# Keys and values of the memory tokens moved from the first attention's filler to the head of a two-block kernel

## The chip, the cores and the metric

The kernel runs on one core of one Trainium2 chip. The metric is the device time of one execution in microseconds (us); of several runs the median counts.

## What is computed

Two transformer blocks follow each other on 512 tokens of width 1024, in float32. The first block has a sliding-window attention with sinks (8 heads), a sparse attention with compressed keys (8 heads), gates, and a convolved feed-forward part. The second block attends to its own tokens in two ways and to 256 memory tokens in a third. Only that third branch touches the memory input, and its keys and values depend on nothing else in the kernel:

```
def mem_branch(mq, mem, mem_norm_g, w_mem_kv, qn_g, kn_g):
    kv = rms_norm(mem, mem_norm_g) @ w_mem_kv
    k = rms_norm(kv[..., :MEM_W].reshape(b, m, MEM_HEADS, MEM_D), kn_g)
    v = kv[..., MEM_W:].reshape(b, m, MEM_HEADS, MEM_D)
```

So the memory keys and values can be made at any time before the second block needs them; the kernel stores them to DRAM and reads them back late. The first block starts with `h = rmsnorm(x, norm_mix)` and products of `h` with parts of one wide weight `w_in`.

## The kernel before

Each float32 product is made as three products of rounded halves. `split` (L97 to L108) and `wsplit` (L125 to L131) round a tile to a high part H on ACT and put the rest L on DVE; `mm3` (L191 to L198) issues H·H, L·H and H·L on TensorE (PE). A weight is loaded by the queue of SP into a tile `raw` (two buffers), and split into `wH` and `wL` (three buffers each) in pieces of 128x1024. A `raw` buffer is free again when the last of its pieces is split.

`block1` (L391) begins with the norm of x: four loads of 512 KB, one square on ACT for each (L411), a short inverse root on DVE (`rsqrt`, L267 to L274), scaling (L414 to L418), 32 transposes on PE (L422), and eight splits into `hH` and `hL` (L107, L108). The transposes use the PSUM tags T, S and O, with two buffers each. Then come three products in a row: the window keys (`dense` at L498), the window queries (L504, four output tiles of 24 matmuls) and the values (`values`, L437). Ahead of the values `mem_load` (L1170) loads the memory (1 MB), takes its norm and transposes it through the tag T alone, 16 transposes and eight splits of 256 columns.

Then `pipeline` (L161) runs the eight window heads. A step of it weaves the scores and the softmax of head i (`swa_a`, L532) with the transposes and the value product of head i-1 (`swa_b`, L571), and with `RS` steps of a filler, `fill1` (L624). A filler step is mostly one `mm3`. The filler begins with `mem_kv` (L1190): 96 matmuls of 256 columns (keys, then values), the norm of the keys, 16 transposes and nine stores. After it come the products of `w_in` for the sparse attention, each with its evacuation, and the two compressions (`compress`, L653).

In the program, a priority scheduler sets each engine's order at build time; every engine then works through its own fixed list and waits on semaphores. The order of the text sets the priorities.

Of the kernel before, what the change touches and what calls it, by code (L numbers as in the profile page):

```python
# [10 lines left out]
F32 = mybir.dt.float32  # L11
# [9 lines left out]
D = 1024  # L21
# [11 lines left out]
POOLL = 14  # L33
RS = 9
RN = 5
# [43 lines left out]
class Build:  # L79
# [76 lines left out]
    @staticmethod  # L156
    def drain(g):
        for _ in g:
            pass

    def pipeline(self, units, filler, rate, extra=(), pool=0):  # L161
# [229 lines left out]
    def block1(self):  # L391
        nc, a, tc, ctx = self.nc, self.a, self.tc, self.ctx
        W = self.rows(a["w_in"][0])
        K8 = [(0, 8)]
# [4 lines left out]
        HH = [hH[:, k] for k in range(8)]  # L399
        HL = [hL[:, k] for k in range(8)]  # L400
        x = a["x"][0].rearrange("(b p) c -> p b c", p=128)
        with tc.tile_pool(name="xp", bufs=1, side="right", reuse_waits="tile") as xp:
            xt = xp.tile([128, 4, D], F32, name="xt")
            ss = xp.tile([128, 4], F32, name="ss")
            junk = xp.tile([128, D], F32, name="junk")
            for b in range(4):
                nc.sync.dma_start(xt[:, b], x[:, b])
            self.constants(xp)
            for i in range(2):
                for b in (2 * i, 2 * i + 1):  # L410
# [61 lines left out]
        def qevac(store):  # L472
# [8 lines left out]
            return f  # L481


        swa = ExitStack()
# [16 lines left out]
        self.leng = nc.vector  # L501
        self.bias_vectors()
        QA = []
        self.dense(W, K8, 0, 512, HH, HL, qevac(QA))  # L504
        mems = ExitStack()
        mem_pool = mems.enter_context(tc.tile_pool(name="mem", bufs=1, side="right", reuse_waits="tile"))
        self.mem_load(mem_pool)
        values()
# [115 lines left out]
        def fill1():  # L624
            yield from self.mem_kv(mem_pool)
            mems.close()
            open_nsa()
# [541 lines left out]

    def mem_load(self, p):  # L1170
        nc, a = self.nc, self.a
        self.sp = p
        mt = p.tile([128, 2, D], F32, tag="mt", name="mt", bufs=1)
        ss = p.tile([128, 2], F32, name="mss")
        self.mH = p.tile([128, 8, 256], F32R, name="memH")
        self.mL = p.tile([128, 8, 256], F32R, name="memL")
        nc.sync.dma_start(mt, a["mem_2"][0].rearrange("(b p) c -> p b c", p=128))
        for b in range(2):
# [678 lines left out]
```

## Time and profile before

| what | value |
|---|---|
| median of 3 runs | 1106.35 us (1102.1 to 1108.65) |
| the profiled execution's own time | 1101.55 us |
| its span in the trace | 1099.8 us |
| PE busy | 1041.1 us (95%), 5425 matmuls |
| DVE busy | 759.9 us (69%) |
| ACT busy | 579.4 us (53%) |
| POOL busy | 269.2 us (24%) |
| DMA traffic | 110.66 MB, mean 101 GB/s |

PE is the engine with the least idle time, but its matmuls are pipelined: a busy time of 394 ns belongs to a matmul that makes room for the next one after some 230 ns. So the distance from one start to the next is read from the timeline, and small gaps do not show as idle time. The profiled execution is faster than the median of the runs by 4.8 us.

### The profile page before, as it was taken

What the parts mean: (1) busy time and instruction counts of PE and PEld (TensorE: products, weight loads), DVE (VectorE), ACT (ScalarE), POOL (GpSimd) and SP (SyncE); (2) the same over time, 40 slices, a digit from 0 to 9 for tenths busy, and PEclk for the clock granted to TensorE, in tenths of its full rate; (3) what the DMA queues carried; (4) which work ended last, traced back from release to release, by engine and by line L of the source; (5) the groups of instructions that cost most, each with busy time, mean ns of one, the idle gap of its engine ahead of it and who ended that gap; (6) DMA issues with size and microseconds to landing.
All of it is one profiled execution on the core that took longest, in us unless ns stands there. A gap on an engine that the chain in (4) does not pass through costs nothing.

```text
span 1099.8 us, 15091 instructions
## 1 busy us (share of the span) xinstructions
PE 1041.1 (95%) x5425; PEld 872.3 (79%) x5425; DVE 759.9 (69%) x1561; ACT 579.4 (53%) x1098; POOL 269.2 (24%) x382
## 2 busy tenths in 40 slices
PE   5999999999999999999999999999999968999798
PEld 4797777878878878888888888888889957776698
DVE  6669884587872655777753477774454898989983
ACT  6557664577772444444432344445537536876540
POOL 4323134232220064000000200001420459332400
PEclk9999999999999999999999999999999989999899
DMA  6845345222114262232222423122324322264212
GB/s 184 275 114 169 101 96 144 44 49 44 49 43 115 77 183 87 77 115 80 89 80 79 153 77 114 59 83 94 110 80 130 97 58 58 62 197 144 71 64 78
DMA packets 105514, 110.66 MB, mean 101 GB/s; under 512 B 5508, under 2 KB 96362, under 8 KB 105440
## 3 DMA queue, kind: packets, MB, share of 16 engines
q1 hardware_dynamic: 101440, 99.07, 31.0%
q0 software_dynamic: 4000, 10.64, 3.2%
q8 instruction: 43, 0.70, 0.3%
q14 instruction: 31, 0.25, 0.1%
HBM read 100.75 MB, written 11.03 MB: 102 GB/s over the span
## 4 chain that ended last, share of the span: by engine, by line
PE 72%; DVE 16%; DMA 5%; ACT 4%; issue 3%; SPq 0%; POOL 0%; ACTq 0%; DVEq 0%; POOLq 0%
PE ps_mm L193 19%; PE ps_mm L197 19%; PE ps_mm L198 19%; DMA raw<-in_w_in 4%; PE ps_S L1247 3%; PE ps_T L383 3%; DVE wL L130 2%; PE ps_O L1278 1%; DVE PTL L102 1%; PE ps_O L1276 1%; DVE e L372 1%; ACT e L374 1%; DVE rt L1101 1%; ACT wH L129 1%; DVE e L1300 1%
## 5 line engine op out<-in xcount | busy, mean ns | idle before, releaser
L129 ACT ACTIVATE wH<-raw 128x1024 fp32r<-128x1024 f32 (+5 forms) x178 | 169.5, 954 | 255.8 <-PE ps_mm L197 207.0
L130 DVE TENSOR_TENSOR wL<-raw,wH 128x1024 fp32r<-128x1024 f32 (+5 forms) x150 | 166.6, 1112 | 112.1 <-ACT wH L129 111.7
L198 PE MATMUL ps_mm<-nH,wL 128*128 128x512 f32 x440 | 173.5, 394 | 5.0 <-POOL wL L130 5.0
L193 PE MATMUL ps_mm<-nH,wH 128*128 128x512 f32 x440 | 173.7, 395 | 0.0
L197 PE MATMUL ps_mm<-nL,wH 128*128 128x512 f32 x440 | 173.4, 394 | 0.0
L374 ACT ACTIVATE e<-e,mn 128x256 f32<-128x256 f32 (+5 forms) x160 | 86.4, 541 | 33.1 <-DVE mn L372 32.0
L198 PEld LDWEIGHTS ps_mm<-nH,wL 128*128 128x128 f32 x440 | 83.3, 189 | 21.9 <-POOL wL L130 5.4
L197 PEld LDWEIGHTS ps_mm<-nL,wH 128*128 128x128 f32 x440 | 83.4, 190 | 16.4
L193 PEld LDWEIGHTS ps_mm<-nH,wH 128*128 128x128 f32 x440 | 83.5, 190 | 16.2
L193 PE MATMUL ps_mm<-hH,wH 128*128 128x512 f32 x232 | 94.2, 406 | 0.5 <-DVE qy L480 0.5
L198 PE MATMUL ps_mm<-hH,wL 128*128 128x512 f32 x232 | 92.2, 398 | 0.0
L197 PE MATMUL ps_mm<-hL,wH 128*128 128x512 f32 x232 | 91.8, 395 | 0.0
L383 PE MATMUL ps_T<-ident,e 128*128 128x128 f32 x368 | 64.9, 283 | 15.4 <-DVE PTL L102 8.6
L130 POOL TENSOR_TENSOR wL<-raw,wH 128x1024 fp32r<-128x1024 f32 (+1 forms) x28 | 60.7, 2167 | 76.1 <-ACT wH L129 64.4
L101 ACT ACTIVATE PTH<-ps_T 128x512 fp32r<-128x512 f32 (+1 forms) x108 | 55.6, 529 | 31.7 <-PE ps_T L383 31.0
L383 PEld LDWEIGHTS ps_T<-ident,e 128*128 128x128 f32 x368 | 45.7, 143 | 32.9 <-DVE PTL L102 9.6
L102 DVE TENSOR_TENSOR PTL<-ps_T,PTH 128x512 fp32r<-128x512 f32 (+1 forms) x108 | 63.8, 606 | 11.3 <-ACT PTH L101 10.7
L193 PE MATMUL ps_mm<-aH,wH 128*128 128x512 f32 x176 | 69.5, 395 | 0.0
L198 PE MATMUL ps_mm<-aH,wL 128*128 128x512 f32 x176 | 69.5, 395 | 0.0
L197 PE MATMUL ps_mm<-aL,wH 128*128 128x512 f32 x176 | 69.5, 395 | 0.0
L965 POOL MEMSET cv<- 128x2 f32 x44 | 4.3, 100 | 237.0 <-DVE cc L969 230.4
L966 DVE TENSOR_TENSOR cv<-ps_mm,rB 128x512 f32<-128x512 f32 x44 | 30.3, 688 | 32.5 <-PE ps_mm L198 31.3
(547 smaller groups left out, 2544.3 us busy)
## 6 DMA issues: line engine op xcount, KB each, us to landing
raw<-in_w_ffn_in SPq DMA_DIRECT2D x20, 1024.0 KB, 5.2
raw<-in_w_in SPq DMA_DIRECT2D x16, 1024.0 KB, 7.1
raw<-in_w_in SPq DMA_DIRECT2D x16, 512.0 KB, 4.1
raw<-in_w_ffn_out SPq DMA_DIRECT2D x8, 768.0 KB, 4.6
raw<-in_w_ffn_out SPq DMA_DIRECT2D x8, 640.0 KB, 4.0
xt<-in_x SPq DMA_DIRECT2D x8, 512.0 KB, 4.9
raw<-in_w_out SPq DMA_DIRECT2D x4, 1024.0 KB, 5.3
raw<-in_w_out SPq DMA_DIRECT2D x8, 512.0 KB, 3.5
```

The source lines that it names most:

```text
L101: nc.scalar.activation(H, src, AF.Copy)
L102: nc.vector.tensor_sub(L, src, f32(H))
L129: self.nc.scalar.activation(H, raw, AF.Copy)
L130: self.leng.tensor_sub(L, raw, f32(H))
L193: ins = mm(ps, wH, xH, start=first, stop=False)
L197: mm(ps, wH, xL, start=False, stop=False)
L198: mm(ps, wL, xH, start=False, stop=last)
L372: nc.vector.tensor_tensor_reduce(e, ps, bias, op0=ALU.add, op1=ALU.min, scale=1.0, scalar=3e38, accum_out=mn)
L374: nc.scalar.activation(e, e, AF.Exp, scale=-1.0, bias=mn, accum_out=sm)
L383: nc.tensor.transpose(ps[:, 128 * i:128 * i + 128], blk, self.ident)
L966: nc.vector.tensor_tensor(v[:, 2:], ps, rB, op=ALU.mult)
L1247: nc.tensor.matmul(ps[:, :n], q[:, 128 * b:128 * b + 128], k[:, :n], start=i == 0, stop=i == len(prods) - 1)
```

## The change

The memory's load is issued ahead of the loads of x (`mem_fetch`). Its norm and the first 16 steps of `mem_kv`, which are all 96 of its matmuls, are written ahead of the norm of x. The rest of `mem_kv` (the norm of the keys, the transposes, the stores) is stepped beside the product for the window queries (`beside_`), which now comes ahead of the window keys. `fill1` starts with the products of `w_in`, and the filler's rate `RS` goes from 9 to 7 steps for each head. The pool of the memory tiles is closed before the window attention's pool opens.

```diff
-RS = 9
+RS = 7
...
+    def beside_(self, g, other):
+
+        for _ in g:
+            next(other, None)
+        self.drain(other)
...
+        mems = ExitStack()
+        mem_pool = mems.enter_context(tc.tile_pool(name="mem", bufs=1, side="right", reuse_waits="tile"))
         with tc.tile_pool(name="xp", bufs=1, side="right", reuse_waits="tile") as xp:
...
+            mt = self.mem_fetch(mem_pool)
             for b in range(4):
                 nc.sync.dma_start(xt[:, b], x[:, b])
             self.constants(xp)
+            self.mem_load(mem_pool, mt)
+            mkv = self.mem_kv(mem_pool)
+            for _ in range(16):
+                next(mkv)
...
+        self.bias_vectors()
+        QA = []
+        self.beside_(self.dense_steps(W, K8, 0, 512, HH, HL, qevac(QA)), mkv)
+        mems.close()
...
         self.leng = nc.vector
-        self.bias_vectors()
-        QA = []
-        self.dense(W, K8, 0, 512, HH, HL, qevac(QA))
-        mems = ExitStack()
-        mem_pool = mems.enter_context(tc.tile_pool(name="mem", bufs=1, side="right", reuse_waits="tile"))
-        self.mem_load(mem_pool)
         values()
...
         def fill1():
-            yield from self.mem_kv(mem_pool)
-            mems.close()
             open_nsa()
...
+    def mem_fetch(self, p):
+        mt = p.tile([128, 2, D], F32, tag="mt", name="mt", bufs=1)
+        self.nc.sync.dma_start(mt, self.a["mem_2"][0].rearrange("(b p) c -> p b c", p=128))
+        return mt
```

What this does to the order of the instructions is shown at three places.

PE, head of the program. Before, the last transposes of x (`xt`) run straight into the first products of the window keys (`hH` and `wH`):

```order
L422 MATMUL ps_T_157<-ident_84,xt_77 128x128 x4
L422 MATMUL ps_S_164<-ident_84,xt_77 128x128 x3
L422 MATMUL ps_O_171<-ident_84,xt_77 128x128 x3
L422 MATMUL ps_T_178<-ident_84,xt_77 128x128 x4
L422 MATMUL ps_S_185<-ident_84,xt_77 128x128 x4
L193 MATMUL ps_mm_220<-hH_72,wH_223 128x512
```

Now the transposes of the memory (`mt`) come first, and its products start between them:

```order
L1200 MATMUL ps_T_139<-ident_89,mt_83 128x128 x2
L435 MATMUL ps_S_343<-ident_89,xt_80 128x128
L435 MATMUL ps_O_350<-ident_89,xt_80 128x128
L435 MATMUL ps_S_364<-ident_89,xt_80 128x128
L435 MATMUL ps_O_371<-ident_89,xt_80 128x128
L1200 MATMUL ps_T_144<-ident_89,mt_83 128x128 x2
L1200 MATMUL ps_T_149<-ident_89,mt_83 128x128 x2
L199 MATMUL ps_mm_174<-wH_177,memH_104 128x256
L203 MATMUL ps_mm_174<-wL_178,memH_104 128x256
```

Four transposes of x stand there; the other 28 stand behind the 96th product of the memory.

ACT, the same part of the program. Before, the splits of x (`hH`) follow the scaling of x with one weight split between:

```order
L414 ACTIVATE xt_77<-xt_77,ss_78 128x1024
L415 ACTIVATE xt_77<-xt_77,ss_78 128x1024
L326 ACTIVATE vec_norm_mix_92<-ps_T_95 128x16
L129 ACTIVATE wH_223<-raw_221 128x1024
L107 ACTIVATE hH_72<-ps_T_136,vec_norm_mix_92 128x512
```

Now they stand behind the evacuation of the memory's values, `mkv` from `ps_mm_235`, the second and last PSUM tile of the memory's products:

```order
L1076 ACTIVATE hsq_452<-mkv_167 128x256
L129 ACTIVATE wH_527<-raw_437 128x1024
L101 ACTIVATE mkv_167<-ps_mm_235 128x4x64
L129 ACTIVATE wH_572<-raw_570 128x1024
L101 ACTIVATE mkv_167<-ps_mm_235 128x4x64
L107 ACTIVATE hH_72<-ps_T_336,vec_norm_mix_97 128x512
```

PE, first window heads. Before, the scores (L549, L550) stand between products of the memory:

```order
L198 MATMUL ps_mm_671<-wH_674,memL_437 128x256
L549 MATMUL ps_S_712<-kaH0_207,qy_326 128x258
L550 MATMUL ps_S_712<-kaL0_209,qy_326 128x258
L193 MATMUL ps_mm_671<-wH_674,memH_436 128x256
L197 MATMUL ps_mm_671<-wL_675,memH_436 128x256
```

Now the products of `h` with `w_in` stand there, with 512 columns:

```order
L561 MATMUL ps_S_908<-kaH0_655,qy_546 128x130
L562 MATMUL ps_S_908<-kaL0_657,qy_546 128x130
L561 MATMUL ps_S_916<-kaH0_655,qy_546 128x258
L562 MATMUL ps_S_916<-kaL0_657,qy_546 128x258
L199 MATMUL ps_mm_892<-hH_72,wH_895 128x512
L203 MATMUL ps_mm_892<-hL_73,wH_895 128x512
L204 MATMUL ps_mm_892<-hH_72,wL_896 128x512
```

From the second compression's last product on (L719 in the kernel before), the order on PE is the same in both programs.

## Rows read from the trace of the kernel before

**Rows 1.** Timeline of the first 20 us (start us, us, instruction [idle before]).

```profile
5.84 1.06 ACT L411 ACTIVATE junk<-xt 128x1024 f32<-128x1024 f32 x1 [0.25 <-DMA xt<-in_x]
9.62 1.06 ACT L411 ACTIVATE junk<-xt 128x1024 f32<-128x1024 f32 x1 [1.34 <-DMA xt<-in_x]
...
11.87 0.48 PE L422 MATMUL ps_T<-ident,xt 128*128 128x128 f32 x1 [3.99 <-ACT xt L414]
12.13 0.42 PE L422 MATMUL ps_S<-ident,xt 128*128 128x128 f32 x1
...
18.33 0.66 PE L422 MATMUL ps_S<-ident,xt 128*128 128x128 f32 x4
18.74 0.48 PE L193 MATMUL ps_mm<-hH,wH 128*128 128x512 f32 x1
```

**Rows 2.** A stretch of 1 us (busy us of PE, PEld, DVE, ACT, POOL; granted clock, DMA share, GB/s).

```profile
9.00:10.00 1.00, 0.00 (x0) 0.00 (x0) 0.33 (x2) 0.38 (x1) 0.78 (x5) 1.00 1.14 345
```

**Rows 3.** Instructions by tile: `mt`, then `memH` (ns min/median/max, first and last start us).

```profile
L1187 PE MATMUL ps_T<-ident,mt x16: 270/273/329, 48.7 to 55.8; 128*128 128x128 f32 x16
L1179 ACT ACTIVATE memH<-mt x2: 1063/1064/1065, 37.4 to 38.6; 128x1024 fp32r<-128x1024 f32 x2
L1183 DVE TENSOR_SCALAR mt<-mt,mss x2: 748/751/754, 44.6 to 45.3; 128x1024 f32<-128x1024 f32 x2
...
L193 PE MATMUL ps_mm<-wH,memH x32: 274/282/365, 69.8 to 84.6; 128*128 128x256 f32 x32
L107 ACT ACTIVATE memH<-ps_T,vec_norm_mix x8: 457/470/476, 50.2 to 56.3; 128x256 fp32r<-128x256 f32 x8
L108 DVE SCALAR_TENSOR_TENSOR memL<-ps_T,vec_norm_mix,memH x8: 475/482/486, 51.5 to 57.4; 128x256 fp32r<-128x256 f32 x8
```

**Rows 4.** Instructions by tile: `raw`, 0 to 50 us (columns as above).

```profile
L129 ACT ACTIVATE wH<-raw x8: 873/1054/1079, 13.0 to 48.8; 128x1024 fp32r<-128x1024 f32 x5, 128x816 fp32r<-128x816 f32 x3
L130 DVE TENSOR_TENSOR wL<-raw,wH x7: 1002/1219/1227, 24.0 to 49.7; 128x1024 fp32r<-128x1024 f32 x4, 128x816 fp32r<-128x816 f32 x3
```

**Rows 5.** Timeline of PE: first window scores, products of the memory.

```profile
69.24 0.33 PE L549 MATMUL ps_S<-kaH,qy 128*128 128x130 f32 x1
...
70.21 0.29 PE L193 MATMUL ps_mm<-wH,memH 128*128 128x256 f32 x1
70.33 0.28 PE L197 MATMUL ps_mm<-wL,memH 128*128 128x256 f32 x1
```

**Rows 6.** Timeline of PE: end of the part in which the orders differ.

```profile
172.28 0.39 PE L198 MATMUL ps_mm<-hH,wL 128*128 128x512 f32 x1
174.53 1.14 PE L719 MATMUL ps_T<-w2v,hv 128*128 128x64 f32 x8 [1.86 <-POOL hv L712]
175.48 0.48 PE L193 MATMUL ps_mm<-hH,wH 128*128 128x512 f32 x1
```

**Rows 7.** Stretches of the window heads (columns as in rows 2).

```profile
69.20:85.35 16.15, 15.68 (x130) 15.24 (x129) 13.45 (x48) 10.98 (x30) 3.00 (x7) 1.00 0.52 139
122.00:135.00 13.00, 11.04 (x55) 9.17 (x54) 8.67 (x22) 8.27 (x18) 1.04 (x2) 0.87 0.47 140
148.00:160.00 12.00, 10.03 (x57) 7.91 (x56) 8.75 (x19) 8.42 (x17) 1.66 (x1) 1.00 0.31 97
sum 106.30, PE 96.56 PEld 79.97 DVE 88.99 ACT 71.87 POOL 27.20; mean PE 10.73 PEld 8.89 DVE 9.89 ACT 7.99 POOL 3.02
```

**Rows 8.** Chain of waits, longest pieces of 69 to 176 us (start us, us, what).

```profile
119.22 7.98 DMA raw<-in_w_in
141.62 8.14 DMA raw<-in_w_in
160.96 9.73 DMA raw<-in_w_in
```

**Rows 9.** Timeline of PE, then a stretch, after the first of these loads.

```profile
129.25 0.52 PE L584 MATMUL ps_O<-PTH,V 128*128 128x256 f32 x1 [1.96 <-ACT PTH L101]
...
131.00:132.00 1.00, 1.00 (x5) 0.81 (x4) 0.40 (x3) 0.00 (x1) 0.00 (x0) 0.50 0.00 0
```

More of the change, by code (lines that the diff above doesn't have):

```diff
@@ L1167, in rope_sines, with mem_load @@
             self.tabs[n] = (cc, sn)
-    def mem_load(self, p):
-        nc, a = self.nc, self.a
+    def mem_fetch(self, p):
+        mt = p.tile([128, 2, D], F32, tag="mt", name="mt", bufs=1)
+        self.nc.sync.dma_start(mt, self.a["mem_2"][0].rearrange("(b p) c -> p b c", p=128))
+        return mt
+    def mem_load(self, p, mt):
+        nc = self.nc
         self.sp = p
-        mt = p.tile([128, 2, D], F32, tag="mt", name="mt", bufs=1)
         ss = p.tile([128, 2], F32, name="mss")
@@ L1176, in mem_load @@
         self.mL = p.tile([128, 8, 256], F32R, name="memL")
-        nc.sync.dma_start(mt, a["mem_2"][0].rearrange("(b p) c -> p b c", p=128))
         for b in range(2):
```

## The prediction

> **What bounds the kernel now.** Read the stretches first: in the window heads PE is busy 96.56 of 106.3 us, DVE 88.99 [rows 7]. From 69.24 us, the first score, to 175.48 us, where the orders of the two programs meet again [rows 5, 6], PE has the least slack, but it waits. The chain of waits names what for: three loads of weights of 7.98, 8.14 and 9.73 us [rows 8]. Each can be issued only when a `raw` buffer has been split on DVE; its own split then stands on ACT ahead of the softmax of a head, and PE waits behind that. The first such wait is 1.96 us long [rows 9]. Then read the timeline of the head: PE has nothing to do until 11.87 us, transposes x, and starts its unbroken stream of products at 18.74 us [rows 1].
>
> All the instructions of before are still there, and from L719 on PE's order is the same. So the change is worth what it does to the time at which PE reaches L719's successor, at 175.48 us before: the head, and the window stage.
>
> **The head.** Memory and x are both wanted from the queue at once. The memory's 1 MB is as much as two blocks of x, so it lands when the second block does now, near 5.8 us [rows 1]. The squares of memory and x follow on ACT in turn: six of 1.06 us, each with a read of some 0.2 us behind it, in the order memory, x, memory, x, x, x. The second one of the memory ends near 9.5 us, the last of x near 13.1 us (the waits for x's blocks fall inside). DVE's inverse root is thirteen small operations in a row, with seven of x's between: about 3.5 us, to 13 us. Two scalings of 0.75 us [rows 3] end at 14.4 us.
>
> Now the memory's transposes. They use only tag T, two buffers, so they go in four rounds of two; a round is a pair of transposes, two ACT splits of 0.47 us and two DVE splits of 0.48 us [rows 3], and the next round waits for DVE. Between rounds stand x's inverse roots and scalings, and weight splits of 1.05 us (ACT) and 1.22 us (DVE) [rows 4]. With these in their order the rounds end on DVE near 16.8, 18.9, 21.7 and 23.8 us. The first weight split is done on ACT at 18.7 us and on DVE at 20.8 us, so products begin, but run on only from 21.8 us. The weights themselves are there: memory, x and both weight chunks are 5.25 MB; at the 0.345 MB per us of [rows 2] after the first 2.6 us that is 17.8 us, and the second chunk is first used at 20 us.
>
> From 21.8 us the 96 products take 0.12 us each [rows 5], 11.5 us, to 33.4 us. I add 1.7 us for the clock: PE idles for more than 2 us between the rounds, and after an idle of 1.96 us the kernel before ran at a granted clock of 0.50, the 1.2 GHz level [rows 9]. The mean of 0.87 over 13 us [rows 7] makes that 13 x 0.13 / 0.5 = 3.4 us at half speed, a loss of 1.7 us. The start of the trace reads otherwise: a transpose at 12.13 us takes 0.42 us, the last ones before 18.74 us take 0.27 us and start 0.13 us apart, (0.66 - 0.27) / 3 [rows 1]. PE had done nothing but transposes in between, so I read there a rise out of the slow level, though the granted column says 1.00 throughout.
>
> The Trainium skill, "TensorE: Matmul & The Clock Gate", in Part 4 on the transpose, says that the full clock does not engage for transposes; by it the first products are slow after any number of transposes, and the 1.7 us stand. By the trace's start, a dense row of transposes would have saved them, and the sum would be 1.7 us lower. The measurement goes against the rule there; I keep the 1.7 us for the gaps alone.
>
> So the products end at 35.1 us. ACT then has two evacuations of the memory's values (0.39 us each, an estimate from the 0.47 us of [rows 3]) and a weight split of 1.05 us ahead of the first split of x (0.69 us, as wide as twice the 0.47 us row less its start), 2.5 us; PE fills them with 20 transposes of x at 0.13 us. The first product of the queries comes at 37.6 us, and x's splits then follow at PE's pace.
>
> Before, at which time was as much work of PE behind it? At 18.74 us it stands where the queries or keys begin, and has still ahead the 96 products (11.5 us) and 16 transposes of the memory (0.13 us each, 2.1 us), while the changed kernel still owes 8 transposes of x (1.0 us): 18.74 + 11.5 + 2.1 - 1.0 = 31.3 us. **The head costs 37.6 - 31.3 = +6.3 us.** The bounds: +2.5 us, if the small operations of two inverse roots overlap, the products run on from 19.7 us and at full clock; +9 us, if every round waits for one weight split more and the loads are late by 2 us.
>
> What else moves here is covered. The nine stores of the memory now stand on SP's queue ahead of the loads for the values, and wait there for ACT; those loads are used some 20 us later, behind 120 products of 512 columns. On POOL the bias strips are made before the window keys' tables; the first strip is read after the values, at about 85 us. The norm of the memory's keys and its 16 transposes go beside the queries, which run PE at its pace with DVE free: nothing.
>
> **The window stage.** It loses the memory's products and transposes, 13.9 us, which are already counted above. Two effects remain.
>
> First, the heads that ran beside these products: from 69.2 to 85.35 us PE idles 0.5 us, in the other 90.15 us 9.3 us [rows 7], for some 6.5 heads, 1.4 us for each. If the first two heads now lose like the others: 2 x 1.4 - 0.5 = **+2.3 us**. (With 7 filler steps for 9, a head has less PE work for cover; the number of steps fits the shorter filler, so no drain of it is left over in either kernel.)
>
> Second, the three loads. Their waits cost 1.96 us and the 1.7 us of slow clock behind it; 12 - 10.03 = 1.97 us in 148 to 160 us; and the 1.86 us before L719 [rows 6, 7, 9], together 7.5 us. In the new order of ACT, 25 rows stand between the split that frees the buffer and the split that wants the second of these loads, where 16 stood: its wait goes, **-2.0 us**. For the first load 12 rows stand for 10: two rows of about 0.5 us off a wait of 1.96 us, and as much again from a shorter slow stretch, **-1.9 us**. For the third 11 for 9, but the last head's softmax now stands behind it: nothing. Bounds: 0 and -7.5 us.
>
> **The sum**: 6.3 + 2.3 - 2.0 - 1.9 = +4.7 us against the profiled 1101.55 us, so 1106.25 us. The runs' median lies 4.8 us above that execution, and it is what the changed kernel's median is set against: 1106.35 + 4.7, about **1111.0 us**, +0.4%. A measurement of this kernel can tell about 0.5%, 5.5 us, from no change; so I forecast no change that can be told.
>
> **Rivals.**
> *The rounds through tag T bind* (slower). If the head costs its +9 us and the stage gives +2.3 - 2.0 back, the sum is +9.3 us, 1115.7 us. For it: two buffers, DVE and ACT with x's work between every pair, and PE at the slow clock. Against it: what stands between the rounds is mostly small operations. It decides when the first query product is later than 38.4 us: there the head costs 7.1 us, and 7.1 + 2.3 - 3.9 reaches 5.5.
> *The window stage runs through* (faster). If all heads run as those from 69.2 to 85.35 us did, with 3% idle, the stage's 9.7 us of idle time become 2.8 us, the 1.7 us of slow clock go too, and with the head at its lower end: 2.5 - 6.9 - 1.7 = -6.1 us, 1100.3 us. For it: the memory's splits leave DVE, and loads are spread wider. Against it: the same weights go through the same two buffers.
> *Only the waits for loads go*: 6.3 + 2.3 - 7.5 = +1.1 us, 1107.5 us; this is no change either and belongs to the forecast.
>
> **Chances and range.** Forecast, within 5.5 us of the median: 0.48. Slower: 0.37; the head's middle alone passes 5.5 us, and what comes back is the less certain part. Faster: 0.15; it needs both ends at once. The range goes from the lower ends, 2.5 - 7.5 = -5.0 us, to the upper ones, 9 + 2.3 = +11.3 us: about 1101.5 to 1117.5 us, with a tenth left out on either side; within the forecast alone it would be 1101.5 to 1111.9 us.
>
> **What would show it.** In the timeline: transposes of the memory from about 13.8 us, products running on from 21.8 us and ending near 35 us, the first query product near 37.6 us; the first window score near 89 us (69.24 + 13.6 + 6.3); the merge behind L719's successor at about 180 us. In the chain of waits: one long load fewer between 90 and 180 us. It is wrong if the query products start before 34 us, if PE's idle time in the window stage is under 5 us or over 14 us, or if anything behind the merge differs by more than 2 us.

## The result, and the profile after

The changed kernel takes **1121.5 us** (median, 1120.1 to 1126.12) against 1107.5 us for the kernel before in the same comparison: a ratio of 1.0141, 95% interval 1.0106 to 1.0176. It is slower by 14 us, where the forecast said 4.7 us, and lies outside the range.

The profiled execution of the changed kernel took 1120.66 us, its span is 1118.9 us, 19.1 us more than the span of 1099.8 us before. The five us between 19.1 and 14.0 are the choice of executions: the profiled one of before lay 6.0 us under its median, this one 0.8 us under. Cut at the places that the prediction names, the 19.1 us lie like this; "equal work" of before is 31.3 us for the first query product and 69.24 + 13.6 = 82.8 us for the first window score, as in the prediction.

| up to | before (equal work) | after | lost in this piece | forecast |
|---|---|---|---|---|
| first query product | 31.3 | 37.94 | 6.6 | 6.3 |
| first window score | 82.8 | 98.42 | **8.9** | **0** |
| product at the merge | 175.48 | 193.50 | **2.4** | **-1.6** |
| end of the span | 1099.8 | 1118.9 | 1.1 | 0 |

PE's timeline in the head (start us, us, instruction [idle before]):

```profile
14.35 1.35 PE L1200 MATMUL ps_T<-ident,mt 128*128 128x128 f32 x4 [6.23 <-DVE mt L1196]
...
20.62 0.58 PE L203 MATMUL ps_mm<-wL,memH 128*128 128x256 f32 x1 [0.73 <-DVE wL L130]
...
25.05 0.41 PE L204 MATMUL ps_mm<-wH,memL 128*128 128x256 f32 x1
25.26 0.33 PE L199 MATMUL ps_mm<-wH,memH 128*128 128x256 f32 x1
25.42 0.28 PE L203 MATMUL ps_mm<-wL,memH 128*128 128x256 f32 x1
...
34.38 0.28 PE L204 MATMUL ps_mm<-wH,memL 128*128 128x256 f32 x1
...
37.94 0.76 PE L199 MATMUL ps_mm<-hH,wH 128*128 128x512 f32 x2 [1.10 <-ACT hH L107]
```

The head came almost as forecast: transposes from 14.35 us (forecast 13.8), products that run on from 20.6 us (21.8) and end at 34.4 us (35.1), and the query products from 37.94 us (37.6). The total is closer than its parts: the products ran on some 1 us sooner than forecast, and some 1 us more passed between the last of them and the first query product. Up to 25.26 us a product starts every 0.21 us, after it every 0.12 us [rows 5].

The loss that nobody had on the list comes next. PE's timeline again:

```profile
64.45 0.39 PE L204 MATMUL ps_mm<-hH,wL 128*128 128x512 f32 x1
71.75 0.76 PE L199 MATMUL ps_mm<-hH,wH 128*128 128x512 f32 x1 [6.91 <-DVE qy L493]
72.31 0.63 PE L203 MATMUL ps_mm<-hL,wH 128*128 128x512 f32 x1
...
76.57 0.40 PE L204 MATMUL ps_mm<-hH,wL 128*128 128x512 f32 x1
```

PE stands still for 6.91 us, in the middle of the query and key products, and then runs 11 products in 4.82 us that take 0.23 us each at full clock: 2.3 us more. 6.91 + 2.3 = 9.2 us cover the 8.9 us of the second piece. The stretches show the granted clock at 0.50 behind it, the 1.2 GHz level (columns as in [rows 2]):

```profile
65.00:70.00 5.00, 0.00 (x0) 0.00 (x0) 1.44 (x2) 1.47 (x2) 0.00 (x0) 0.97 0.96 253
70.00:75.00 5.00, 3.25 (x8) 2.60 (x9) 3.50 (x6) 2.66 (x4) 3.58 (x11) 0.50 0.35 78
```

PE waits for DVE's split of a query tile, DVE for ACT. ACT's timeline shows why, then come the issues on SP's queue and on POOL's:

```profile
54.15 0.60 ACT L1239 ACTIVATE mkt<-ps_T 128x512 fp32r<-128x512 f32 x1 [3.08 <-DMA mkTl_d<-mkt]
...
56.92 0.59 ACT L492 ACTIVATE qy<-ps_mm 64x512 fp32r<-64x512 f32 x1 [0.75 <-DVE qy L493]
67.61 0.88 ACT L129 ACTIVATE wH<-raw 128x816 fp32r<-128x816 f32 x1 [10.10 <-DMA raw<-in_w_in]
68.52 0.59 ACT L492 ACTIVATE qy<-ps_mm 64x512 fp32r<-64x512 f32 x1
```

```profile
55.14 0.52 SPq L1241 DMA_DIRECT2D mkTl_d<-mkt  x1
55.76 9.29 SPq L455 DMA_DIRECT2D raw<-in_w_in  x6
```

```profile
48.02 4.23 POOL L361 DMA_DIRECT2D rep<-rvec  x8 [1.03 <-DMA rvec<-rv]
```

ACT stood 10.10 us before the first split of the **values'** weights (128x816). Their products come only after the keys; but the split stands on ACT ahead of the evacuations of two query tiles (L492), and PE needs those buffers for its next product. Their load could be issued only at 55.76 us, behind the stores of the memory's keys, and landed at 67.5 us: eight bias strips of 384 KB had been issued on POOL from 48.02 us. Two suspects, then: the store queue and the strips.

The window stage, first score to merge (columns as in [rows 2]); then the end of the stage on PE, and the two long loads that are left in the chain of waits (start us, us, what):

```profile
98.42:193.50 95.08, 84.06 (x459) 69.62 (x457) 78.33 (x185) 61.08 (x136) 27.39 (x33) 0.95 0.39 102
```

```profile
98.42 0.33 PE L561 MATMUL ps_S<-kaH,qy 128*128 128x130 f32 x1
...
184.59 0.30 PE L703 MATMUL ps_T<-ident,gx 62*128 62x62 f32 x2 [3.89 <-DVE gx L699]
...
193.50 0.48 PE L199 MATMUL ps_mm<-hH,wH 128*128 128x512 f32 x1
```

```profile
127.99 6.64 DMA raw<-in_w_in
...
170.41 10.25 DMA raw<-in_w_in
```

Of the three loads of [rows 8] the middle one is gone from the chain, as forecast; the last one got longer, 10.25 us for 9.73, and PE waits 3.89 us behind it where it waited 1.86 us [rows 6]. A wait of 1.70 us behind DVE, at 162.08 us, is new. PE idles 11.0 us in the stage (95.08 - 84.06), 9.7 us before (106.30 - 96.56 in the sum line of [rows 7], which covers the whole stage and not only the three stretches shown there), where the stage held the memory's 13.6 us of products as well, and the mean clock is 0.95.

### The profile page after: what moved, and what is told of

Read it like the earlier page. It is cut to its first block, busy times and chain, and to the rows that moved or that the text cites. A ratio compares the mean times of both kernels' runs of the same rounds, so it can differ in the third digit from the quotient of the medians.

```text
span 1118.9 us, 15079 instructions
## 1 busy us (share of the span) xinstructions
PE 1047.4 (94%) x5425; PEld 879.5 (79%) x5425; DVE 754.8 (67%) x1561; ACT 577.8 (52%) x1098; POOL 270.8 (24%) x382
## 3 DMA queue, kind: packets, MB, share of 16 engines
q0 software_dynamic: 4000, 10.64, 3.4%
## 4 chain that ended last, share of the span: by engine, by line
PE 71%; DVE 15%; DMA 6%; ACT 5%; issue 3%; SPq 0%; POOL 0%; ACTq 0%; DVEq 0%; POOLq 0%
PE ps_mm L199 19%; PE ps_mm L204 18%; PE ps_mm L203 18%; DMA raw<-in_w_in 4%; PE ps_T L389 3%; PE ps_S L1260 3%; DVE wL L130 2%; PE ps_O L1291 1%; PE ps_O L1289 1%; ACT wH L129 1%; DVE rt L1111 1%; DVE PTL L102 1%; DMA xt<-in_x 1%; DVE e L378 1%; ACT e L380 1%
## 5 line engine op out<-in xcount | busy, mean ns | idle before, releaser
L130 DVE TENSOR_TENSOR wL<-raw,wH 128x1024 fp32r<-128x1024 f32 (+5 forms) x150 | 166.5, 1111 | 123.7 <-ACT wH L129 123.3
L199 PE MATMUL ps_mm<-hH,wH 128*128 128x512 f32 x232 | 96.7, 418 | 9.5 <-DVE qy L493 6.9
L130 POOL TENSOR_TENSOR wL<-raw,wH 128x1024 fp32r<-128x1024 f32 (+1 forms) x28 | 60.5, 2162 | 78.0 <-ACT wH L129 66.3
L199 PEld LDWEIGHTS ps_mm<-hH,wH 128*128 128x128 f32 x232 | 45.3, 195 | 16.7 <-issue 7.3
```

What stands on the lines that cost most here:

```text
L130: self.leng.tensor_sub(L, raw, f32(H))
L199: ins = mm(ps, wH, xH, start=first, stop=False)
```

## The experiments

A table first; the columns are the median, the ratio to the kernel before with its 95% interval, then from the profile the first window score, the start of the second compression's last products (L719 before, L729 or L739 in the others: just ahead of the merge) and PE's longest waits up to there, behind 24 us. The ratio compares with runs of the kernel before that were made beside that run. In runs that change the steps (e3, e4, e23, e27, e28, e29) other work stands ahead of the last products, so that column compares only runs with the same steps.

| run | us | ratio | first score | last products | PE's longest waits |
|---|---|---|---|---|---|
| changed kernel | 1121.5 | 1.0141 (1.0106 to 1.0176) | 98.4 | 192.7 | 6.91, 3.89 |
| e1 stores on ACT's queue | 1121.6 | 1.0126 (1.0076 to 1.0177) | 96.2 | 189.5 | 2.92, 2.38, 3.49 |
| e2 four buffers | 1120.8 | 1.0124 (1.008 to 1.0167) | 97.9 | 192.4 | 6.37, 4.00 |
| e5 strips late | 1120.7 | 1.0105 (1.0052 to 1.0159) | 91.2 | 193.2 | 4.05, 4.09 |
| e12 strips early | 1121.6 | 1.0138 (1.0095 to 1.018) | 101.0 | 193.3 | 10.64, 3.08 |
| e13 early, keys first | 1121.0 | 1.0128 (1.0092 to 1.0163) | 99.2 | 193.1 | 7.28, 2.07, 3.79 |
| e19 strips in the gap | 1116.0 | 1.008 (1.0054 to 1.0105) | 93.7 | 186.6 | 2.29, 3.81 |
| e20 and stores on ACT | 1116.3 | 1.0073 (1.0048 to 1.0098) | 95.2 | 188.8 | 2.03, 3.71 |
| e22 and sinks on SP | 1112.8 | 1.0062 (1.0037 to 1.0086) | 93.5 | 186.1 | 1.65, 3.21 |
| e23 and 8 steps | 1109.7 | 1.0029 (1.0007 to 1.0051) | 91.7 | 178.9 | 1.57, 5.97 |
| e27 and 2 query steps | 1104.1 | 0.9979 (0.9959 to 0.9999) | 91.4 | 171.1 | 1.94, 1.40 |
| e28 and 10 query steps | 1107.5 | 1.0013 (0.9992 to 1.0035) | 91.8 | 183.1 | 1.61, 3.45 |
| e9 x first | 1119.7 | 1.0103 (1.0056 to 1.015) | 94.9 | 190.0 | 2.78, 3.87 |
| e21 queries first | 1119.4 | 1.011 (1.0073 to 1.0147) | 96.4 | 192.0 | 6.75, 3.65 |
| e3 changed, 9 steps | 1122.8 | 1.0136 (1.01 to 1.0172) | 98.2 | 189.5 | 6.03, 5.35, 3.47 |
| e4 before, 7 steps | 1106.3 | 0.9991 (0.9969 to 1.0012) | 69.7 | 172.2 | 0.81 |
| e29 before, 2 query steps | 1102.2 | 0.9975 (0.9948 to 1.0002) | 73.8 | 174.2 | 4.13, 2.81 |

**The store queue (e1, e2).** e1 issues the eight stores on ACT and gives their tile four buffers; e2 has the buffers alone.

```
-            kt = p.tile([128, S], F32R, name="mkt", bufs=2)
+            kt = p.tile([128, S], F32R, name="mkt", bufs=4)
-            nc.sync.dma_start(f32(self.mkT[:, h]), f32(kt[:, :256]))
-            nc.sync.dma_start(f32(self.mkTl[:, h]), f32(kt[:, 256:]))
+            nc.scalar.dma_start(f32(self.mkT[:, h]), f32(kt[:, :256]))
+            nc.scalar.dma_start(f32(self.mkTl[:, h]), f32(kt[:, 256:]))
```

> Edit: the changed kernel, with the eight stores of the memory's keys issued on ACT's queue instead of SP's, and four buffers for their tile instead of two. Theory (queue): the loads of the values were issued only at 55.76 us, behind these stores, and their split stands on ACT ahead of the evacuations of the queries, so PE idled 6.91 us and then ran at half clock from 71.75 to about 76.5 us (2.4 us lost). Without the stores on that queue the loads go out near 38 to 45 us, the idle time and the half clock go, the first window score comes near 89.5 us instead of 98.42, and the time falls by about 9 us, to 1110 to 1114 us. Rival (strips): the eight bias strips of POOL fill the DMA engines, and the wait stays at 4 us or more, 1117 to 1121 us. Rival (ACT): issuing the stores costs ACT so much that the evacuations are late in another place; the first score at 95 us or later.

> Edit: the changed kernel with four buffers instead of two for the tile of the memory's keys, stores left on SP's queue. Theory (queue): only the wait for a store's landing (3.08 us on ACT before 54.15) goes, so the loads of the values go out some 3 to 3.5 us earlier, near 52.3 us; PE's idle time of 6.91 us falls to 3 to 4 us, it still drops to half clock, and the time falls by about 3 us, to 1117 to 1119 us. Rival (strips): the landing is set by the strips' transfers and not by the issue: the load lands near 67 us as now, and the time stays at 1120 to 1122 us.

Measured: no change in time in either. The chain of waits of e1 at the values' load, ACT's split of it, and PE behind it:

```profile
51.72 1.24 DVE wL L130
52.97 12.80 DMA raw<-in_w_in
```

```profile
67.64 0.89 ACT L129 ACTIVATE wH<-raw 128x816 fp32r<-128x816 f32 x1 [10.18 <-DMA raw<-in_w_in]
71.80 0.47 PE L199 MATMUL ps_mm<-hH,wH 128*128 128x512 f32 x1 [2.92 <-DVE qy L493]
```

The load now goes out as soon as DVE has split its buffer's last weights, 2.8 us sooner, and lands no sooner: it takes 12.8 us and more, and ACT's split starts at 67.64 us where it started at 67.61 us. The queue theory falls as the main cause; the store queue held the load back by 2.8 us, and the buffer itself came free only at 52.96 us. That leaves the transfer.

**The strips, moved (e5, e12, e13).** e5 makes them behind the window keys, e12 in the head behind the constants, e13 there too, with the window keys made ahead of the queries. The first added line below is that of e12, the last that of e5.

```
+            self.bias_vectors()
...
-        self.bias_vectors()
         QA = []
...
         self.leng = nc.vector
+        self.bias_vectors()
         values()
```

> Edit: the changed kernel with the bias strips made after the window keys, where they stood before the change, and the stores left as they are. Theory (queue): the loads still go out near 55 us, but without the strips' 3 MB beside them they take 4 to 5 us and not 9.84, so they land near 61 us: PE's idle time falls from 6.91 to under 2 us, and 1112 to 1117 us. Rival (the strips are no cause): the load takes 9 us and more all the same, idle time 6 us or more, 1119 to 1122 us. If the strips come too late for the first window heads, PE or DVE waits for them near 90 to 100 us and some of it is given back.

> Edit: the changed kernel with the bias strips made right behind the constants, in the head, instead of in front of the queries. Theory (strips): what held PE for 6.91 us was not the store queue (without it the values' load was issued 2.8 us sooner and landed at the same 67 us) but the 3 MB of the strips, which went to the DMA engines from 48 us, 4 us ahead of this load. With the strips gone from there the load lands near 58 us, PE's idle time before the first window score falls to under 1 us and its half clock after it goes: first score near 89.5 us, if the strips cost the head nothing, and 1112 to 1115 us. Rival (order on ACT): the split of the load stands ahead of the query evacuations, and its buffer comes free only at 52 to 55 us, so 2 to 4 us of idle time stay: 93 us or later, 1116 to 1119 us. Rival (the window stage eats it): the first score comes near 90 us, but the end of the part with different orders is not earlier by more than 4 us.

> Edit: as the run with early strips, and the window keys made before the queries again, as in the kernel before, so that the values' loads get their buffers while the queries run. Theory (strips): as the early strips alone, within 2 us, because the load had slack already. Rival (order on ACT): only this one takes PE's idle time before the first window score to under 1 us, and it is faster than the early strips alone by 2 to 4 us. In both the head's loss of 6.6 us and the window stage's 2.4 us are left: 1111 to 1115 us.

Measured: the time is the same in all three, and that is the finding: each removes the wait of 6.91 us and gets another. e5 shows the cause most directly, as it changes nothing but the place of the strips and leaves the stores on SP's queue. ACT's split of the values' weights, then PE:

```profile
60.09 0.89 ACT L129 ACTIVATE wH<-raw 128x816 fp32r<-128x816 f32 x1 [2.56 <-PE ps_mm L203]
```

```profile
95.94 0.80 PE L199 MATMUL ps_mm<-hH,wH 128*128 128x512 f32 x1 [4.05 <-ACT gate L466]
```

The six parts of the values' loads take 3.2 to 5.5 us from issue to landing, where they took 7.0 to 10.2 us in the changed kernel. They also go out from 51.6 us on, not 55.76, because ACT waits 0.71 us for a store to land where it waited 3.08 us: the strips held up the stores as well. ACT splits 7.5 us sooner and no longer waits for the load, and the first score comes at 91.2 us for 98.4 us. Then PE stands 4.05 us in the window stage, behind a load of 10.70 us that meets the strips there, and runs behind it at a granted clock of 0.62 (97 to 102 us): the stage takes 7.7 us more, and the gain is gone. In e12 the first load of query weights meets them (chain of waits, then PE):

```profile
22.91 17.80 DMA raw<-in_w_in
```

```profile
47.76 0.79 PE L199 MATMUL ps_mm<-hH,wH 128*128 128x512 f32 x1 [10.64 <-ACT hH L107]
```

The same 1 MB took 8.01 us in the changed kernel, with the strips not yet under way. e13 gave no gain from the keys' place because the early strips cost it 7.28 and 2.07 us first. So in these three runs and in the changed kernel the 3 MB of strips cost PE a wait of 4 to 11 us wherever they met a load that PE was about to need. The Trainium skill, "DMA: Bandwidth & Descriptors", section "Issuing engines are not separate DMA queues", says that transfers started by different engines run on the same DMA engines and interleave; the rows agree: strips on POOL's queue and loads on SP's, 8.01 us against 17.80 us.

**The strips in a gap (e19), then with the other two collisions taken away (e20, e22).** In e19 the strips' vectors are computed in the head and held back on POOL by a sum with zeros taken from the memory's first evacuated product; e20 adds the stores on ACT, e22 also loads the attention sinks on SP.

```
+    def bias_strips(self, p, gate):
+        z = p.tile([8, RL], F32, name="rvz")
+        nc.gpsimd.tensor_scalar(z, gate, 0.0, None, op0=ALU.mult)
+        for i, sb in enumerate(self.rvs):
+            nc.gpsimd.tensor_tensor(sb, sb, z, op=ALU.add)
+            nc.gpsimd.dma_start(rvec[8 * i:8 * i + 8], sb)
...
-        self.bias_vectors()
+        self.bias_strips(mem_pool, self.kn0)
...
-        nc.gpsimd.dma_start(skb, bass.AP(tensor=sk.tensor, ...
+        nc.sync.dma_start(skb, bass.AP(tensor=sk.tensor, ...
```

> Edit: the changed kernel with the same bias strips made earlier, in the gap of the transfers: their vectors are computed in the head, and a copy of zeros taken from the memory's first evacuated product holds them back on POOL until about 30 us, so that the strips go out near 34 us instead of 48. Theory (strips collide with a load that PE needs at once): at 48 us they met the values' load (6.91 us of idle time), at 18 us the first query load (10.64 us); at 34 us all loads that are under way have 8 us and more of slack. The idle time near 65 to 72 us falls under 2 us, and none over 2 us comes in its place; first window score near 91 us instead of 98.4, and the time falls by 6 to 8 us, to 1113 to 1116 us. Rival (the volume binds: every load of the first 70 us waits for the one before it, and the strips' 9 us are lost wherever they lie): first score at 96 us or later, 1119 us or more.

> Edit: the run with the strips in the gap, and in addition the stores of the memory's keys on ACT's queue with four buffers. Theory (strips and store queue together): each hides the other; with the strips away the store queue still holds the values' load back by 3 us, so this run is faster than the strips in the gap alone by 1 to 3 us: first window score near 89.5 us, 1111 to 1114 us. Rival (the store queue does nothing): both within 1 us of each other in the first window score.

> Edit: as the run with the strips in the gap and the stores on ACT's queue, and the small load of the attention sinks on SP's queue instead of POOL's. Theory (collisions ahead of the window stage): in that run DVE, in its order, stood before the sinks' scaling until a 4.05 us load on POOL's queue had landed at 68 us, and PE idled 2.03 us behind it. With it gone PE's idle time between 56 us and the first window score is under 1 us, the first score comes near 91.5 us, and what the strips, stores and this load cost ahead of the window stage is all back: 1111 to 1114 us, the kernel before plus the head's 6.6 us. Rival (something else there binds next): a wait of 2 us or more at another place between 56 and 80 us, first score at 94 us or later, no faster than 1116 us.

The strips go out at 41.09 us in e19 (not 34: the two sums take 3.76 us on POOL, and the landing of the vectors 3.92 us), and the kernel gains 5.5 us. A wait of 2.29 us stays. In e19 it comes from the stores: ACT stands before the next tile of the memory's keys until a store has landed, with a query evacuation behind it (ACT, then PE):

```profile
57.53 0.60 ACT L1250 ACTIVATE mkt<-ps_T 128x512 fp32r<-128x512 f32 x1 [5.25 <-DMA mkTl_d<-mkt]
```

```profile
62.25 0.47 PE L199 MATMUL ps_mm<-hH,wH 128*128 128x512 f32 x1 [2.29 <-DVE sink L520]
```

With four buffers and the stores on ACT's queue (e20) that wait is gone, and another of 2.03 us stands in its place. DVE's timeline in e20:

```profile
68.00 0.27 DVE L523 TENSOR_SCALAR sink<-skb 128x8 f32<-128x8 f32 x1 [2.59 <-DMA skb<-in_attn_sinks]
68.30 0.69 DVE L503 TENSOR_TENSOR qy<-ps_mm,qy 64x512 fp32r<-64x512 f32 x1
```

DVE stands, in its order, before a scaling that waits for a load of 4 KB, and the query split that PE needs stands behind it. In e22 that is gone and the time is 1112.8 us, within the 1111 to 1114 us expected; its first score, 93.5 us, is 2 us later than expected: ACT stood 3.48 us in the issue of the stores and PE 1.65 us behind it. That is this execution, not the edit: in e23, whose engines have the same orders up to the first score, the same four issues held ACT for 1.56 us and the first score came at 91.7 us.

With these collisions gone the median is 8.7 us less than the changed kernel's. That it is so near the 8.9 us of the second piece is in part luck: from first query product to first score the profiled execution of e22 takes 54.6 us and that of e23 52.7 us, where the changed kernel's took 60.5 us, so 5.8 and 7.8 us come back there. From e19 to e20 the time did not change, but not because the store queue does nothing: one wait of 2 us went and another came. The first scores lie 1.4 us apart, where the rival allowed 1 us.

**The head (e9, e21).** Both load and norm x first and make the memory beside the queries, with the stores on ACT; e21 fetches the memory's rows only behind the first step of the queries, where e9 has the line below.

```
-            mt = self.mem_fetch(mem_pool)
             for b in range(4):
                 nc.sync.dma_start(xt[:, b], x[:, b])
+            mt = self.mem_fetch(mem_pool)
...
-            for _ in range(16):
-                next(mkv)
```

> Edit: x is loaded, normed and transposed first, then the memory's norm and transposes; all products and the key norm of the memory run beside the query products; the stores of the keys on ACT's queue with four buffers. Theory: the head's loss of 6.6 us (the first query product at 37.94 us, where equal work stood at 31.3 us) goes, because PE starts its products near 18.7 us as before the change; with the stores' wait gone too, only the loss in the window stage (2.4 us) and what lies behind it (1.1 us) are left: 1109 to 1113 us, about the kernel before plus 3 us. Rival (loads): six chunks of weights now go through two buffers in the first 60 us, and PE waits for them instead: idle time of 4 us or more before the first window score, 1114 us or more.

> Edit: x is loaded, normed and transposed first, then the first query weights; the memory is loaded only then, and its norm, transposes and products run beside the query products; stores on ACT's queue, strips as in the changed kernel. Theory (head): the 6.6 us that the changed kernel lost before its first query product go, since PE starts them near 19 us; with 3 us of idle time elsewhere the first window score comes near 87 us, and the time is that of the kernel before plus 3 to 6 us, 1110 to 1113 us. Rival (loads): with 5 MB more to come in the first 60 us the loads set the pace whatever comes first: idle time of 6 us or more before the first score, 92 us or later, and 1116 us or more.

The queries start early in both (e9: 22.77 us), but e9 waits 2.89, 0.75 and 2.78 us ahead of the first score and e21 6.75 us in one piece. The numbers are those that the rival of both gave; its reason, that the loads set the pace, is not what the rows show. In e21 the memory had landed by 22.03 us, when ACT takes its square. Then the memory's inverse root, in DVE's order between two weight splits and two query splits, lasts until 31.77 us, and the memory's transposes stand ahead of the next products on PE (DVE, then PE):

```profile
31.80 1.42 DVE L1196 TENSOR_SCALAR mt<-mt,mss 128x1024 f32<-128x1024 f32 x2
```

```profile
32.66 1.30 PE L1200 MATMUL ps_T<-ident,mt 128*128 128x128 f32 x4 [6.75 <-issue]
```

In e9 ACT works without a pause from the memory's second square to the first weight split (20.63 to 22.72 us), and PE waits 2.89 us for that. So in both runs the order of the small work on DVE and ACT held PE, and the head's 6.6 us weren't to be had in these two ways; no run shows that they can't be had.

**The window stage (e3, e4, e23, e27, e28, e29).** The number of steps, `RS`, and the query steps between the last keys and the second compression. `RS` is 8 in e23, e27 and e28, 9 in e3 and, in the kernel before, 7 in e4; the query steps are 2 in e27 and e29 and 10 in e28:

```
-RS = 7
+RS = 8
...
-            for _ in range(6):
+            for _ in range(2):
                 next(qg)
```

> Edit: the changed kernel with 9 filler steps for each window head, as before the change, instead of 7. Theory: the steps fit the shorter filler, so 9 would use it up two heads early: the last heads lose their cover, 1.4 us of idle time each, and the time rises by 2 to 4 us, to 1123 to 1126 us. Rival (7 steps are what the window stage lost on): the stage gets 2 us or more shorter than its 94.3 us, and the time falls to 1117 to 1120 us.

> Edit: the kernel before with 7 filler steps for each window head instead of 9. Theory: the filler with the memory's products needs 9; with 7 some 16 steps are left over and run behind the last head, where they have no softmax to cover but also lose nothing as PE runs on: 1106 to 1112 us. Rival (the number of steps decides how heads and loads meet): more than 5.5 us either way, 1101 us or less or 1113 us or more.

> Edit: the run before this one with 8 filler steps for each window head instead of 7. Theory (order in the window stage): the longest wait there, 3.7 to 4.0 us in front of the second compression, comes because ACT stands before the split of the third load with the last head's softmax and the compression's tanh behind it; with 8 steps the split falls into another head, the wait falls under 2 us or goes, and the time from the first window score to the end of that part falls by 2 us or more from 93 to 94 us. Rival (the load decides, as long as 10 us whatever stands behind it): the wait shows up at another product, 3 us or more, and the time of the part changes by less than 1.5 us.

> Edit: as the run with 8 steps, and 2 query steps instead of 6 ahead of the second compression, so that the third load's split stands on ACT behind the compression's tanh and the softmax of a head instead of ahead of them. Theory (order on ACT): PE's wait of 5.97 us in front of the compression's transposes goes; what is left is a wait for the load itself of 3 us or less, at a product; the part from the first window score to the merge takes 82 to 85 us (87.2 with 6 steps), and the time is 1104 to 1107 us, level with the kernel before. Rival (the load's own 10 us decide): the wait is 5 us or more at another place and the part takes 87 us or more, 1109 us.

> Edit: as the run with 8 steps, and 10 query steps instead of 6 ahead of the second compression: the third load's split still stands on ACT one row ahead of the compression's tanh. Theory (order on ACT): the wait in front of the compression's transposes stays, 3 us or more, and the time is 1108 to 1112 us. Rival (the load's own duration decides): by the query steps that come ahead of the load, PE has more to do while it lands, the wait falls under 2 us, and the part takes 85 us or less.

> Edit: the kernel before (memory beside the window heads, 9 steps, strips as they were), with 2 query steps instead of 6 ahead of the second compression. Theory (the gain of the last run but one lies in the order on ACT, not in making the memory first): in the kernel before, 6 to 2 takes the wait of 1.86 us and the load's wait behind it away as well, and it gains 2 to 4 us: 1103 to 1105 us. Rival (it needs the memory out of the window stage): with the memory's products in the same filler the second compression lies elsewhere, and the time stays within 1.5 us of the kernel before or rises.

The steps alone are worth nothing that can be told in either kernel (e3, e4); e3's 1122.8 us lie just under the 1123 to 1126 us expected. On top of e22, 8 steps gained 3.2 us, though the wait that I wanted away grew to 5.97 us: both readings missed. What the 3.2 us come from isn't shown. SP's and ACT's rows of e23, then of e27:

```profile
154.81 2.60 SPq L122 DMA_DIRECT2D raw<-in_w_in  x2
```

```profile
165.18 1.06 ACT L129 ACTIVATE wH<-raw 128x1024 fp32r<-128x1024 f32 x1 [5.39 <-DMA raw<-in_w_in]
```

```profile
150.79 0.37 SPq L122 DMA_DIRECT2D raw<-in_w_in  x1
164.25 0.37 SPq L122 DMA_DIRECT2D raw<-in_w_in  x1
```

```profile
158.64 1.06 ACT L129 ACTIVATE wH<-raw 128x1024 fp32r<-128x1024 f32 x1 [1.81 <-DMA raw<-in_w_in]
...
160.60 0.40 ACT L706 ACTIVATE gt<-gt 62x256 f32<-62x256 f32 x1
```

My expectation of e27 gave the wrong reason: the split still stands ahead of the compression's tanh (L706, 160.60). What changed is that the two loads of 1 MB no longer go out together. In e23 both `raw` buffers come free within 2.6 us, the two loads share the transfer, and the first takes 10.29 us; in e27 they are 13 us apart, and the one that ACT wants takes 7.83 us. The wait of PE there falls from 5.97 to 1.3 us at most, and the time to 1104.1 us; the part up to the last products took 79.7 us, under the 82 to 85 us expected. In e28 the two go out together again (10.44 us) and PE waits 3.45 us, now before a head's value product; the time, 1107.5 us, lies half a us under the range expected. That the distance of the two loads is the cause is argued from these three runs; no run changes that distance with all else equal.

e29 asks whose gain this is. The kernel before with the same edit takes 1102.2 us, 0.9975 (0.9948 to 1.0002). PE waits there too, 4.13 and 2.81 us, at other places than in the kernel before, so that it isn't shown what its gain, if it is one, comes from. So the best version with the memory first is level with, not ahead of, the kernel before with the same small edit: making the memory first brings nothing that could be told.

## Why the prediction was wrong

**The head: right.** First query product forecast at 37.6 us, measured at 37.94; the loss 6.6 us for 6.3. The half clock was sized rightly too: 17 products from 20.62 to 25.26 us at 0.21 us for 0.12 are 1.6 us, where I took 1.7. The granted column says 1.00 throughout those us, as in the start of the trace before; the durations say otherwise. Whether the gaps between the rounds or the transposes themselves kept the clock low isn't told apart here. By the rule of the Trainium skill, "TensorE: Matmul & The Clock Gate", Part 4 on the transpose, the first products would be slow as well, so that this run speaks neither for nor against it. The slow rival, "the rounds through tag T bind", would have needed the first query product behind 38.4 us, and falls; so does the fast one, "the window stage runs through", with 11.0 us of idle time where it had 2.8.

**"What else moves here is covered": the step that failed.** The prediction said of the stores on SP's queue that "those loads are used some 20 us later, behind 120 products of 512 columns", and costed the bias strips at nothing because the first strip is read late. Both sentences look at when PE uses the bytes. Neither asks who touches the load first (ACT's split, in ACT's order ahead of evacuations that PE does wait for) and neither asks what the strips' 3 MB do to the loads beside them. Before, strips and values' loads overlapped too, and the loads took up to 13.6 us to land; but they had been issued from 26.34 and 33.78 us on, with the keys made first, and PE waited 0.45 us. The change moved the loads behind the memory's and left the strips where the loads now are. This term, put at nothing, measured 8.9 us. It stood in no bound of the sum, so that the range of 1101.5 to 1117.5 us could not hold the result. That the strips are the cause of the wait is shown by moving them (e5, e12, e19); that the place of the split on ACT passes the wait on to PE is read from the timeline, and no run moves that split alone. Of the prediction's signs only the first window score, near 89 us in the forecast and 98.42 us in the trace, pointed at this piece; none of the three that were to show it wrong came, as none looked there.

**The window stage: -1.6 forecast, +2.4 measured.** The second load's wait went, as forecast. The first load's did not fall as far as forecast: waits of 0.80 and 0.91 us stand where 1.96 us stood. The third, put at nothing, costs 2.0 us more (3.89 for 1.86). And the clock fell more often: the mean of 0.95 over 95.08 us is 4.8 us at (1 - clock) x time; before it was 0.98 over 106.24 us, 2.1 us (each good to half a us, as the clock has two digits). These 2 to 3 us had no term of their own. Together the terms come to more than the 4.0 us that were missed, so some other term must have come out lower than forecast; no run tells which.

**Behind the merge:** 1.1 us, inside the 2 us named; no run tells what it is.

**The forecast as a whole.** "No change that can be told" had 0.48, "slower" 0.37. The slower side was right, by a mechanism that wasn't on the list. With the collisions taken away (e22) the kernel stands at 1112.8 us, 1.7 us over the forecast of 1111.0.

Not settled: what the 1.1 us behind the merge are, and what makes the clock fall at 144 us (below). A third `raw` buffer, which would test the pairing of loads directly, wasn't tried.

## What to carry to other kernels

When an edit moves a load or a store, follow each transfer to the first instruction that touches it, and ask what stands behind that instruction on its engine; the engine that touches the data first stops first, and what stands behind it stops with it. Lay the transfers of all queues on one axis, by bytes and time: large transfers that nobody is waiting for are only free while every load beside them has slack, and reordering work can take that slack without touching them. A term costed at nothing needs an upper bound like any other, and it belongs into the range.

## What the runs showed of the hardware

Two loads of 1 MB from one queue that went out within 3 us of each other took 10.25 us (changed kernel, at 170.41 us) and 10.29 us (e23); one that went out with no other near it took 6.64 us (at 127.99 us).

TensorE's clock fell without a long wait. In the changed kernel (columns as in [rows 2]):

```profile
142.00:143.00 1.00, 0.52 (x5) 0.52 (x5) 0.97 (x2) 0.19 (x1) 0.00 (x0) 1.00 0.00 0
143.00:144.00 1.00, 0.30 (x4) 0.19 (x3) 0.95 (x3) 0.63 (x2) 0.00 (x0) 1.00 0.00 0
144.00:145.00 1.00, 1.00 (x4) 0.58 (x4) 0.97 (x5) 1.00 (x2) 0.00 (x0) 0.91 0.02 8
145.00:146.00 1.00, 0.77 (x4) 0.35 (x3) 1.00 (x1) 0.39 (x2) 0.86 (x2) 0.50 0.00 0
...
151.00:152.00 1.00, 1.00 (x5) 0.82 (x4) 1.00 (x2) 0.20 (x2) 1.00 (x1) 0.68 0.00 0
```

PE's longest single wait from 142 to 146 us was 0.70 us, but it was busy for 0.82 of the 2 us before 144; then it ran at the 1.2 GHz level until 151.4 us or so. I had looked for the slow clock only behind waits of about 2 us.

A transfer issued by ACT costs ACT time. With the stores on its queue (e22) ACT's timeline reads:

```profile
51.12 1.16 ACTq L1252 DMA_DIRECT2D mkTl_d<-mkt  x1
52.32 1.44 ACTq L1251 DMA_DIRECT2D mkT_d<-mkt  x1
53.80 0.83 ACTq L1252 DMA_DIRECT2D mkTl_d<-mkt  x1
54.68 0.72 ACT L1241 ACTIVATE mks<-mkv 128x256 fp32r<-128x256 f32 x2 [3.48 <-issue]
```

The three issues here took 0.83 to 1.44 us each, and ACT lost 3.48 us with them and the one ahead (0.34 us); the four of the next pair of tiles, at 57 to 59 us, took 0.33, 0.44, 1.23 and 0.45 us. In e23 the same first four took 0.42 to 0.51 us each:

```profile
54.22 0.73 ACT L1241 ACTIVATE mks<-mkv 128x256 fp32r<-128x256 f32 x2 [1.56 <-issue]
```

What sets the price isn't shown.
